# Gathered rows used by VectorE behind the split of the next block's U, with six gather buffers instead of five

## The chip, the core and the metric

The kernel runs on one core of a Trainium2 chip. The metric is the device time of one execution in microseconds. The kernel before has a median of 1936.19 us over three runs (1919.65 to 1936.87). The trace is of one more execution, with a time of 1931.02 us. TensorE (PE in the rows) multiplies, VectorE (DVE) does elementwise work, ScalarE (ACT) casts and evaluates functions, GpSimd (POOL) issues the gathers, and SyncE (SP) issues the plain loads.

## The reference

One decoder block on 512 tokens of width 1024: adaLN and RMSNorm, differential attention and mLSTM side by side, an output projection, and then a PEER feed-forward. Only the last matters here:

```
q = (h @ w_q) per head; v_top, i_top = top_k(q . sub_keys, 16) on two halves of 128 keys
sc, sel = top_k(all 256 sums, 16);  idx = the chosen experts (of 16384);  gate = softmax(sc)
act = gelu(einsum('thed,td->the', U[idx], h))
y   = einsum('the,thed->td', gate * act, V[idx])
```

Every token has 8 heads times 16 choices, so 128 rows of U and 128 rows of V, each row 1024 numbers wide. The output is x + gt2 * y, normalised.

## The kernel before

The 512 tokens are four tiles of 128. The feed-forward treats them in two ways.

**Dense, for tiles 1 to 3 (384 tokens).** All 16384 experts are computed in 128 blocks of 128 experts. `up(n1)` loads a 128x1024 block of U (`raw_U`, L990), ScalarE casts it to a rounded part `hi_U` (L991), VectorE subtracts to get the rest `lo_U` (L992, the split of U), and TensorE does 24 matmuls of 384 columns, three for each of eight slices: hi by hi (L1000), hi by the activations' low part (L1001), lo by hi (L1002). ScalarE takes the gelu (`ga`, L1004). The second half of a block loads and splits a block of V in the same way (`hi_V`, `lo_V`, helper `split`, L137 and L138), VectorE multiplies `ga` by the routing weights (L1031), `ga` is split too (`ahi`, `alo`), and TensorE does 18 matmuls of 512 columns (L1046), which add up in PSUM over all 128 blocks. `hi` and `lo` tiles of U and V have two buffers each, `ga` has 32, so the U half may run up to 32 blocks ahead of the V half.

**Gathered, for tile 0 (128 tokens).** The experts' rows are fetched instead: one indirect DMA on GpSimd's queue (L925) brings, for choice s, one row of 1024 floats to each of the 128 partitions (512 KB). With a row of U, VectorE takes the dot product with the token's activations (L931). After all 128 there is one gelu and one multiplication by the gates, and then each row of V is added to `yg`, weighted (L941). There are 256 gathers, 128 of U and then 128 of V. `gstep` spreads them over blocks 16 to 126 of the dense loop, two or three to a block (256 over 111 blocks). The choices of tile 0 are made by `select_gather` at blocks 3 and 5, with scratch tiles from the same pool of buffers as the gathers (tag `g`, `NGB` buffers of 4 KB to a partition). At the end, a last low part and three tiles of the closing normalisation come from that pool as well.

**What sets the order.** The program is written in one order, and a planner (`schedule_with_timeline_sim=True`) simulates the engines with modelled durations and writes out each engine's list: an instruction that is ready in its simulation goes ahead of one that isn't, and among ready ones the one that was written earlier. On the chip each engine works through its list in order, and waits in front of an instruction whose inputs are late. `tc.issue_after(x)` orders those instructions of its block which run on the engine of `x` behind `x`; it adds no semaphore. In `up`, GpSimd copies one column of `lo_U` (`pace`, L994), and the gathers of that block stand behind this copy on GpSimd's list, so they don't start before the block's split. Nothing orders their uses on VectorE but their data and the planner.

Of the kernel before, what the change touches and what calls it, by code (L numbers as in the profile page):

```python
# [10 lines left out]
F32 = mybir.dt.float32  # L11
# [6 lines left out]
OP = mybir.AluOpType  # L18
# [10 lines left out]
KEYS = 128  # L29
# [11 lines left out]
    (O_QA + hp * 256,), (O_KA + hp * 256,), (O_VA + hp * 256,), (O_QM + hp * 128, O_KM + hp * 128),  # L41
    (O_VM + hp * 256,), (O_OM + hp * 256,), (O_GM + hp * 256,), (O_GA + hp * 256,))]
NGA = 32
NGB = 5
QB = 1
RB = 6
STB = 2
# [14 lines left out]
def block_kernel(ctx: ExitStack, tc: tile.TileContext, a, out, dbg=None):  # L62
    nc = tc.nc
    dbg = dbg or {}
    V, A, G, T = nc.vector, nc.scalar, nc.gpsimd, nc.tensor
# [58 lines left out]
    def wtiles(kind, name, raw=None):  # L124

        return (raw or wpool.tile([P, D], F32, tag=f"w_raw{kind}", bufs=2, name=f"raw_{name}"),
                wpool.tile([P, D], F32R, tag=f"w_hi{kind}", bufs=2, name=f"hi_{name}"),
                wpool.tile([P, D], F32R, tag=f"w_lo{kind}", bufs=2, name=f"lo_{name}"))
# [15 lines left out]
    def acc_tile(name):  # L144
        return ps_acc.tile([P, 512], F32, tag="acc", name=name)
# [83 lines left out]
    with tc.tile_pool(name="start", bufs=1, side="right") as sp:  # L229
# [55 lines left out]
        for half in range(2):  # L285
# [4 lines left out]
            for k in ks:  # L290
# [3 lines left out]
                                                       op=OP.subtract)  # L294
# [423 lines left out]
    NS = NH * TOPK  # L718
# [204 lines left out]
    def gather(src, s):  # L923
        t_ = gpool.tile([P, D], F32, tag="g", bufs=NGB, name="gath")
        G.indirect_dma_start(out=t_, out_offset=None, in_=src,  # L925
                             in_offset=bass.IndirectOffsetOnAxis(ap=idx0[:, s:s + 1], axis=0))
        return t_

    def gather_u(s):
        u = gather(a["U"], s)  # L930
        V.scalar_tensor_tensor(junk2, u, 1.0, hrow, op0=OP.mult, op1=OP.mult, accum_out=act[:, s:s + 1])  # L931
        if s == NS - 1:
            A.activation(act, act, AF.Gelu)
            V.tensor_tensor(act, act, gate0, op=OP.mult)

    def gather_v(s):
        v = gather(a["V"], s)
        if s == 0:
            V.tensor_scalar(yg, v, act[:, 0:1], None, op0=OP.mult)
        else:  # L940
            V.scalar_tensor_tensor(yg, v, act[:, s:s + 1], yg, op0=OP.mult, op1=OP.add)  # L941

    def select_gather(h0):

        room = gpool.tile([P, D], F32, tag="g", bufs=NGB, name="room")
        s0 = gpool.tile([P, D], F32, tag="g", bufs=NGB, name="s0")
        used, made = [0], {}

        def mk(name, shape, dt=F32):
            n = int(np.prod(shape[1:])) * (2 if dt == F16 else 4) // 4  # L950
            if name in ("ge", "stp"):
                t_, n0 = gpool.tile([P, D], F32, tag="g", bufs=NGB, name=name), 0
            elif name == "cand":
# [19 lines left out]
        for h in range(4):  # L973
            for p in range(2):
# [2 lines left out]
        V.scalar_tensor_tensor(idx0[:, gs], idg.rearrange("p h k -> p (h k)"), float(KEYS),  # L977
                               idl.rearrange("p h k -> p (h k)"), op0=OP.mult, op1=OP.add)

    gsteps = [(gather_u, s) for s in range(NS)] + [(gather_v, s) for s in range(NS)]  # L980
    h_hi, h_lo = h2_hi[:, :, d0:d0 + XT], h2_lo[:, :, d0:d0 + XT]

    def gstep(n1):
        return min(2 * NS, max(0, (n1 - G0) * 2 * NS // (KEYS - GE - G0)))

    def up(n1):

        raw, hi, lo = wtiles(0, f"U{n1}", gpool.tile([P, D], F32, tag="rawU", bufs=NRU, name="raw_U")
                             if n1 >= NGA + 4 else None)
        nc.sync.dma_start(raw, a["UT"][n1])  # L990
        A.copy(hi, raw)  # L991
        V.tensor_tensor(lo, raw, hi.bitcast(F32), op=OP.subtract)  # L992
        pace = dp.tile([P, 1], F32, tag="pace", bufs=4, name="pace")
        with tc.issue_after(G.tensor_copy(pace, lo[:, 0:1].bitcast(F32)).ins):  # L994
            for f, s in gsteps[gstep(n1):gstep(n1 + 1)]:
                f(s)
        ps = acc_tile("act")[:, 0:XT]
        for k in range(KD):
            ks = slice(k * P, (k + 1) * P)
            T.matmul(ps, hi[:, ks], h_hi[:, k], start=(k == 0), stop=False)  # L1000
            T.matmul(ps, hi[:, ks], h_lo[:, k], start=False, stop=False)  # L1001
            T.matmul(ps, lo[:, ks], h_hi[:, k], start=False, stop=(k == KD - 1))  # L1002
        ga = dp.tile([P, XT], F32, tag="ga", bufs=NGA, name="ga")
        A.activation(ga, ps, AF.Gelu)  # L1004
        return ga
# [3 lines left out]
    for n1 in range(KEYS):  # L1009
        if n1 in SG:  # L1010
            select_gather(4 * SG.index(n1))
        for u in range(n1, n1 + 1) if n1 < KEYS - SKEW else range(n1, KEYS) if n1 == KEYS - SKEW else ():
            gas[u] = up(u)
# [18 lines left out]
        if n1 == KEYS - 1:  # L1032
            both = gpool.tile([P, D], F32R, tag="g", bufs=NGB, name="ahl")
            ahi, alo = both[:, 0:XT], both[:, XT:2 * XT]
# [15 lines left out]

    gt2 = gpool.tile([P, D], F32, tag="g", bufs=NGB, name="gt2")
    nc.sync.dma_start(gt2, gt2_dram.partition_broadcast(P))
# [81 lines left out]
```

## Time and profile before

| | |
|---|---|
| runs | 1936.19 us median, 1919.65 to 1936.87 |
| the profiled execution | 1931.02 us, span 1929.2 us |
| TensorE busy | 1814.1 us, 94% |
| VectorE busy | 1428.4 us, 74% |
| ScalarE busy | 811.1 us, 42% |
| GpSimd busy | 685.8 us, 36% |
| DMA | 404 MB, 210 GB/s on average |
| gathers of U, of V | 1052.6 to 1409.9 us, 1411.1 to 1890.3 us |

Times in rows count from the start of the span. The share of busy time is a mean over stages with different limits, so the stretch in which the gathers run has to be read apart from the rest. A bracket at the end of a row of the timeline is the time for which the engine stood idle in front of that instruction, and what ended it.

### The profile page before, as it was taken

To read this page: it belongs to the slowest core of one execution; us is meant where nothing else is said; L and a number is where in the kernel's file an instruction comes from. 1 tells how busy PE (TensorE), PEld (TensorE's weight loads), DVE (VectorE), ACT (ScalarE), POOL (GpSimd) and SP (SyncE) were. 2 spreads that over 40 slices of the span, in tenths; PEclk is the share of its full clock that TensorE was granted. 3 is DMA by queue.
4 is the path that set the end of the run, shared out by engine and by line. 5 is a ranking of instruction groups with operands and counts; after the bars stand their busy time and mean duration, and the time that the engine had idled before them with its cause. 6 is when DMAs were issued, how large, how long until landed. Compare 5 with 4: busy or idle time off the path is not lost.

```text
span 1929.2 us, 28915 instructions
## 1 busy us (share of the span) xinstructions
PE 1814.1 (94%) x10751; PEld 1632.3 (85%) x10751; DVE 1428.4 (74%) x2732; ACT 811.1 (42%) x1359; POOL 685.8 (36%) x608
## 2 busy tenths in 40 slices
PE   5999899899998998999699999999999899999997
PEld 4989799798986888999688888899898788888886
DVE  7664746645556799999889888887776667776777
ACT  5565464463562423555434333333333233333332
POOL 2523325234135310331001664565433433334333
PEclk8999999999999999999799999999999999999999
DMA  8422414314222233366794999999986887787883
GB/s 283 129 69 81 138 59 158 112 63 148 71 88 98 75 102 99 117 239 247 265 302 153 339 355 349 317 337 336 323 285 247 276 299 274 273 295 246 321 283 132
DMA packets 160283, 404.26 MB, mean 210 GB/s; under 512 B 14471, under 2 KB 63368, under 8 KB 160142
## 3 DMA queue, kind: packets, MB, share of 16 engines
q1 hardware_dynamic: 117026, 240.91, 38.6%
q0 software_dynamic: 36864, 134.23, 19.0%
q10 hardware_dynamic: 6252, 27.28, 3.6%
q8 instruction: 84, 1.38, 0.3%
q14 instruction: 57, 0.47, 0.1%
HBM read 373.52 MB, written 28.84 MB: 209 GB/s over the span
## 4 chain that ended last, share of the span: by engine, by line
PE 58%; DVE 18%; DMA 9%; ACT 5%; issue 5%; POOL 4%; SPq 0%; DVEq 0%; POOLq 0%; ACTq 0%
PE y L1046 20%; PE act L1002 7%; PE act L1000 7%; PE act L1001 7%; DMA gath<-V,idx 4%; DMA ada_w<-ada_w 3%; POOL gath L925 2%; DVE lo_U L992 2%; DVE ada_acc L219 1%; DVE lo_V L138 1%; PE wps L876 1%; PE wps L877 1%; DVE ga L699 1%; ACT p L489 1%; DVE gm L701 1%
## 5 line engine op out<-in xcount | busy, mean ns | idle before, releaser
L1002 PE MATMUL act<-h_hi,lo_U 128*128 128x384 f32 x1024 | 347.1, 339 | 16.9 <-DVE lo_U L992 16.7
L1000 PE MATMUL act<-h_hi,hi_U 128*128 128x384 f32 x1024 | 345.0, 337 | 2.6 <-ACT ga L1004 2.2
L1001 PE MATMUL act<-h_lo,hi_U 128*128 128x384 f32 x1024 | 344.3, 336 | 0.0
L994 POOL COPY pace<-lo_U 128x1 f32<-128x1 f32 x128 | 99.9, 782 | 572.8 <-DVE lo_U L992 572.1
L941 DVE SCALAR_TENSOR_TENSOR yg<-gath,act,yg 128x1024 f32<-128x1024 f32 x127 | 163.0, 1283 | 111.2 <-DMA gath<-V,idx 110.6
L1046 PE MATMUL y<-lo_V,ahi 128*128 128x512 f32 x762 | 241.2, 397 | 2.6 <-DVE lo_V L138 2.6
L137 ACT CAST hi_V<-raw_V 128x1024 fp32r<-128x1024 f32 x128 | 134.3, 1050 | 245.9 <-PE y L1046 207.3
L1046 PE MATMUL y<-hi_V,alo 128*128 128x512 f32 x762 | 233.9, 395 | 1.0 <-DVE alo L138 1.0
L1046 PE MATMUL y<-hi_V,ahi 128*128 128x512 f32 x762 | 222.4, 397 | 6.0 <-ACT ahi L137 4.2
L925 POOL DMA_INDIRECT gath<-U,idx x128 | 177.1, 1383 | 130.1 <-DVE junk L931 99.3
L1002 PEld LDWEIGHTS act<-h_hi,lo_U 128*128 128x128 f32 x1024 | 192.8, 188 | 25.3 <-DVE lo_U L992 20.6
L1000 PEld LDWEIGHTS act<-h_hi,hi_U 128*128 128x128 f32 x1024 | 192.9, 188 | 8.5 <-ACT ga L1004 3.1
L1001 PEld LDWEIGHTS act<-h_lo,hi_U 128*128 128x128 f32 x1024 | 192.7, 188 | 4.3
L138 DVE TENSOR_TENSOR lo_V<-raw_V,hi_V 128x1024 fp32r<-128x1024 f32 x128 | 155.8, 1219 | 41.9 <-ACT hi_V L137 39.0
L991 ACT CAST hi_U<-raw_U 128x1024 fp32r<-128x1024 f32 x128 | 134.2, 1049 | 111.4 <-PE act L1001 98.6
L137 ACT CAST ahi<-ga 128x384 fp32r<-128x384 f32 x127 | 65.0, 512 | 271.0 <-DVE ga L1031 140.3
L1046 PEld LDWEIGHTS y<-hi_V,alo 128*128 128x128 f32 x762 | 142.5, 187 | 35.4 <-DVE alo L138 1.9
L1046 PEld LDWEIGHTS y<-lo_V,ahi 128*128 128x128 f32 x762 | 142.8, 188 | 35.0 <-DVE lo_V L138 3.6
L992 DVE TENSOR_TENSOR lo_U<-raw_U,hi_U 128x1024 fp32r<-128x1024 f32 x128 | 156.4, 1222 | 19.4 <-ACT hi_U L991 13.3
L1046 PEld LDWEIGHTS y<-hi_V,ahi 128*128 128x128 f32 x762 | 142.0, 189 | 33.3 <-ACT ahi L137 4.8
L925 POOL DMA_INDIRECT gath<-V,idx x128 | 149.4, 1167 | 35.3 <-issue 31.5
L931 DVE SCALAR_TENSOR_TENSOR junk<-gath,hrow 128x1024 bf16<-128x1024 f32 x128 | 156.0, 1219 | 4.4 <-DMA gath<-U,idx 3.5
(465 smaller groups left out, 4134.2 us busy)
## 6 DMA issues: line engine op xcount, KB each, us to landing
raw_U<-UT SPq DMA_DIRECT2D x128, 512.0 KB
raw_V<-V SPq DMA_DIRECT2D x128, 512.0 KB
ada_w<-ada_w SPq DMA_DIRECT2D x96, 256.0 KB
W_dram<-st ACTq DMA_DIRECT2D x24, 960.0 KB
W<-W_dram SPq DMA_DIRECT2D x60, 384.0 KB
raw_wq<-wq SPq DMA_DIRECT2D x16, 512.0 KB
raw_q<-w_in SPq DMA_DIRECT2D x8, 512.0 KB
raw_k<-w_in SPq DMA_DIRECT2D x8, 512.0 KB
```

The source lines that it names most:

```text
L137: A.copy(hi, src)
L138: eng.tensor_tensor(lo, src, hi.bitcast(F32), op=OP.subtract)
L925: G.indirect_dma_start(out=t_, out_offset=None, in_=src, in_offset=bass.IndirectOffsetOnAxis(ap=idx0[:, s:s + 1], axis=0))
L931: V.scalar_tensor_tensor(junk2, u, 1.0, hrow, op0=OP.mult, op1=OP.mult, accum_out=act[:, s:s + 1])
L941: V.scalar_tensor_tensor(yg, v, act[:, s:s + 1], yg, op0=OP.mult, op1=OP.add)
L991: A.copy(hi, raw)
L992: V.tensor_tensor(lo, raw, hi.bitcast(F32), op=OP.subtract)
L994: with tc.issue_after(G.tensor_copy(pace, lo[:, 0:1].bitcast(F32)).ins):
L1000: T.matmul(ps, hi[:, ks], h_hi[:, k], start=(k == 0), stop=False)
L1001: T.matmul(ps, hi[:, ks], h_lo[:, k], start=False, stop=False)
L1002: T.matmul(ps, lo[:, ks], h_hi[:, k], start=False, stop=(k == KD - 1))
L1046: T.matmul(ys[d][j], l[:, tsl], r[:, j * 512:(j + 1) * 512], start=(m == 0 and i == 0), stop=(m == KEYS - 1 and i == 2))
```

## The change

The gather of a row and its use on VectorE are taken apart. `up(n1)` now issues its block's gathers and puts them into a list, `landing`. The next `up` empties that list right after its own split of U, inside `issue_after` on that split, so a block's uses stand behind the next block's `lo_U` on VectorE's list. In the last block the list is emptied once more at the end. The pool `g` gets a sixth buffer.

```diff
-NGB = 5
+NGB = 6
...
-    def gather_u(s):
-        u = gather(a["U"], s)
+    def use_u(s, u):
         V.scalar_tensor_tensor(junk2, u, 1.0, hrow, op0=OP.mult, op1=OP.mult, accum_out=act[:, s:s + 1])
...
-    def gather_v(s):
-        v = gather(a["V"], s)
+    def use_v(s, v):
...
-    gsteps = [(gather_u, s) for s in range(NS)] + [(gather_v, s) for s in range(NS)]
+    gsteps = [(f, n, s) for f, n in ((use_u, "U"), (use_v, "V")) for s in range(NS)]
+    landing = []
...
-        V.tensor_tensor(lo, raw, hi.bitcast(F32), op=OP.subtract)
+
+        with tc.issue_after(V.tensor_tensor(lo, raw, hi.bitcast(F32), op=OP.subtract).ins):
+            while landing:
+                f, s, t_ = landing.pop(0)
+                f(s, t_)
         pace = dp.tile([P, 1], F32, tag="pace", bufs=4, name="pace")
         with tc.issue_after(G.tensor_copy(pace, lo[:, 0:1].bitcast(F32)).ins):
-            for f, s in gsteps[gstep(n1):gstep(n1 + 1)]:
-                f(s)
+            for f, n, s in gsteps[gstep(n1):gstep(n1 + 1)]:
+                landing.append((f, s, gather(a[n], s)))
+        if n1 == KEYS - 1:
+            while landing:
+                f, s, t_ = landing.pop(0)
+                f(s, t_)
```

## Rows read from the trace of the kernel before

**Rows 1.** Stretches of gathered U and V: length, busy us (count) by engine, clock, DMA.
```profile
1052.00:1411.00 359.00, 357.77 (x1726) 313.51 (x1725) 297.10 (x445) 130.98 (x177) 196.84 (x159) 1.00 0.93 329
1411.00:1900.00 489.00, 472.97 (x2353) 423.48 (x2352) 344.01 (x354) 161.70 (x223) 180.29 (x184) 1.00 0.81 280
```

**Rows 2.** The same stretches, line 1046 alone (PE, PEld).
```profile
1052.00:1411.00 359.00, 238.03 (x969) 180.28 (x967) 1.00 0.93 329
1411.00:1900.00 489.00, 241.97 (x993) 185.26 (x994) 1.00 0.81 280
```

**Rows 3.** Timeline of TensorE: start, duration; L1000 starts every third matmul.
```profile
1508.38 0.34 PE L1000 MATMUL act<-h_hi,hi_U 128*128 128x384 f32 x1
...
1512.55 0.33 PE L1000 MATMUL act<-h_hi,hi_U 128*128 128x384 f32 x1
```

**Rows 4.** The chain of work that ended last, in order of time: start, duration.
```profile
1526.25 1.23 DVE lo_U L992
1528.14 2.30 POOL gath L925
1530.74 8.50 DMA gath<-V,idx
1540.54 1.22 DVE lo_V L138
...
1547.93 4.19 PE y L1046 x18
```

**Rows 5.** Waits from 1411 to 1900 us: total us, times, longest.
```profile
DVE yg L941 <- DMA gath<-V,idx: 110.6, 66, 5.1
...
PE act L1002 <- DVE lo_U L992: 12.8, 7, 4.7
```

**Rows 6.** Timeline of VectorE: start, duration, idle before it.
```profile
1513.06 1.28 DVE L941 SCALAR_TENSOR_TENSOR yg<-gath,act,yg 128x1024 f32<-128x1024 f32 x1
...
1539.34 1.28 DVE L941 SCALAR_TENSOR_TENSOR yg<-gath,act,yg 128x1024 f32<-128x1024 f32 x1 [3.39 <-DMA gath<-V,idx]
...
1541.67 1.22 DVE L992 TENSOR_TENSOR lo_U<-raw_U,hi_U 128x1024 fp32r<-128x1024 f32 x1
...
1544.94 1.23 DVE L992 TENSOR_TENSOR lo_U<-raw_U,hi_U 128x1024 fp32r<-128x1024 f32 x1 [0.45 <-ACT hi_U L991]
...
1549.47 1.29 DVE L941 SCALAR_TENSOR_TENSOR yg<-gath,act,yg 128x1024 f32<-128x1024 f32 x1 [1.71 <-DMA gath<-V,idx]
```

**Rows 7.** Timeline of ScalarE, the cast ahead of the split at 1541.67.
```profile
1533.99 1.04 ACT L991 CAST hi_U<-raw_U 128x1024 fp32r<-128x1024 f32 x1
```

**Rows 8.** Timeline of TensorE around its longest wait in this stretch.
```profile
1537.88 0.34 PE L1001 MATMUL act<-h_lo,hi_U 128*128 128x384 f32 x1
1542.95 0.69 PE L1002 MATMUL act<-h_hi,lo_U 128*128 128x384 f32 x1 [4.73 <-DVE lo_U L992]
```

**Rows 9.** The 3.3 us after that wait, columns as in the first group.
```profile
1543.00:1546.30 3.30, 3.30 (x10) 3.30 (x11) 2.28 (x4) 1.85 (x3) 2.37 (x4) 0.50 0.88 309
```

**Rows 10.** Timeline of GpSimd: two gathers of V.
```profile
1513.34 2.30 POOL L925 DMA_INDIRECT gath<-V,idx  x1 [0.16 <-issue]
...
1543.56 0.97 POOL L925 DMA_INDIRECT gath<-V,idx  x1 [0.16 <-issue]
```

**Rows 11.** The gathers by tile: issue in ns (min/median/max), first and last start.
```profile
L925 POOL DMA_INDIRECT gath<-U,idx x128: 932/1282/4195, 1052.6 to 1409.9; - x128
...
L925 POOL DMA_INDIRECT gath<-V,idx x128: 933/963/3903, 1411.1 to 1890.3; - x128
```

**Rows 12.** Splits of U in each stretch: busy us, mean ns, idle before.
```profile
L992 DVE TENSOR_TENSOR lo_U<-raw_U,hi_U 128x1024 fp32r<-128x1024 f32 x32 | 39.1, 1221 | 8.2 <-PE act L1002 3.3 <-ACT hi_U L991 2.9 <-issue 1.1
L992 DVE TENSOR_TENSOR lo_U<-raw_U,hi_U 128x1024 fp32r<-128x1024 f32 x56 | 68.3, 1220 | 11.7 <-ACT hi_U L991 10.4 <-PE act L1002 1.0 <-issue 0.3
```

**Rows 13.** Waits from 1052 to 1411 us: total us, times, longest.
```profile
POOL gath L925 <- DVE junk L931: 99.3, 78, 6.5
...
ACT hi_V L137 <- DMA raw_V<-V: 10.4, 4, 7.4
```

## The prediction

> **What bounds the kernel now.** I read the stretches first, then TensorE's pace, then the chain of waits, then who waits there, and last the timelines.
>
> By stretches, TensorE is busy 357.8 of 359 us while rows of U are gathered, and 473.0 of 489 us while rows of V are [rows 1]. Busy isn't full pace, so I count matmuls. A U block's 24 take 4.17 us at full pace (eight steps of three [rows 3]), a V block's 18 take 4.19 us [rows 4]. In the V stretch 993 of 2353 matmuls are line 1046 [rows 1, 2]: 55.2 V blocks and 56.7 U blocks, 231.2 + 236.3 = 467.5 us. So TensorE loses **21.5 us** of 489. In the U stretch 969 and 757 give 225.6 + 131.5 = 357.1 us, a loss of 1.9 of 359. The kernel is bound by TensorE, and what a change of the gathers can give back there is at most 23 us, 1.2%.
>
> The chain shows what costs those 21.5 us: a circle [rows 4]. A split of U ends, GpSimd issues that block's gathers behind it (2.30 us for one), the row lands 8.50 us later, and only then come the next split of V and the next split of U. VectorE takes its list in order, so a use that stands ahead of a split holds the split until the row is there. This costs VectorE 110.6 us in 66 waits, and TensorE 12.8 us in seven waits for `lo_U` [rows 5]. In the worst one VectorE waited 3.39 us in front of the use at 1539.34; the split of U at 1541.67 [rows 6] had its cast ready from 1535.0 [rows 7]; TensorE, which had started its last matmul at 1537.88, stood until 1542.95 [rows 8]. Afterwards the granted clock was 0.50, the lower level of 1.2 GHz, for 3.3 us with ten matmuls [rows 9], which take 10 x 0.174 = 1.7 us at full pace [rows 3]: 1.6 us more. That use belongs to the block whose split stands at 1526.25 [rows 4], so it is exactly one that the change puts behind the split at 1541.67.
>
> **The change part by part.**
>
> *Uses behind the next split.* No instruction is added or taken away; on VectorE 256 uses move, and what stands behind them moves up. In the case above the split of V is free to start after its own cast and the split of U from 1535.0; two splits of 1.22 us [rows 6] end by about 1537.5, and TensorE needs the result at 1538. The wait goes. I let all seven go, with the clock's part: 12.8 + 1.6 = **14.4 us**. Above it lies the whole loss of 21.5 us, below it nothing; I take 14.4 because the rows name its cause, while the other 7.1 us are shorter gaps for which `lo_U` isn't named.
>
> *What stays.* The splits come in pairs: 1541.67 and 1544.94 [rows 6]. A use of the first one's rows already stands behind the second split: the gather issued at 1543.56 [rows 10] is used at 1549.47 after a wait of 1.71 us [rows 6], 5.9 us after its issue. The change can't move that one. Only the second block of each pair, about 28 of 56 [rows 12], gets its rows a whole pair's time to land, 16.7 us (2 x 8.36). What is late next is this first use, with the splits of V behind it.
>
> *The wait that is added.* It is an order on VectorE alone, without a semaphore. Behind a late split now stand its predecessor's uses; who waits for these are the gathers that need their buffers. Two blocks in a row hold at most five (256 over 111 blocks), so with six the next block's gathers always find one. I cost it at 0, covered by VectorE's 145 us of idle time in the V stretch (489 - 344 [rows 1]).
>
> *GpSimd's list.* The gathers stay behind `pace`, 256 of them before and after, no DMA is added, and SyncE's list doesn't change. Cost 0.
>
> *Six buffers in the U stretch.* Here the order isn't binding: of 128 splits 56 + 32 come later [rows 12], so 40 were done when block 16's gathers started at 1052.6 [rows 11]; the uses lag far behind. But GpSimd waited 99.3 us for buffers [rows 13], and the sixth lets gathers go up to 6/5 as fast. They move 128 x 0.524 MB in 359 us, 187 of 329 GB/s [rows 1]; a fifth more makes 366 GB/s, and the DMA share 0.93 would go to 1.03. The next loads of V could then come late. From above: ScalarE's waits for `raw_V`, 10.4 us [rows 13], twice as long and all on TensorE, +10 us. From below: this stretch's loss gone, -1.9 us. I take 0, since TensorE lost just 1.9 us here with the DMA this full.
>
> *Scratch and tail.* A sixth buffer may let the second `select_gather` start sooner, and the closing loads too. Between 0 and 2 us of gain, as the tail after the last gather's use is short; I take 0.
>
> **Sum.** 1931.0 - 14.4 = 1916.6 us against the profiled execution. That one stands 5.2 us below the median of the runs shown, so the same step from the median gives 1921.8. I predict the middle, **1919 us**, 0.9% below the median. One per cent, 19.4 us, is about what a measurement of this kernel can tell from no change: the bounds are 1916.8 and 1955.6.
>
> **The rivals.**
>
> *The whole loss goes.* If rows that land late feed the shorter gaps too, TensorE gets 23.4 us back: 1907.6, from the median 1912.8, say 1910. For it speaks that nothing else in the V stretch is near full; against it that half of the uses don't move.
>
> *Given back.* Uses now follow a split directly, which is when GpSimd, released by `pace`, issues the block's gathers. A gather's issue has a median of 0.963 us in the V stretch and 1.282 us in the busier U stretch [rows 11], and the one at 1513.34 beside the use at 1513.06 took 2.30 us [rows 6, 10]. If each gather took 2.30 - 0.96 = 1.34 us more, a block's rows (2.31 on average) would land 3.1 us later, and for the first block of each of 28 pairs VectorE would wait 87 us more. Of its waits 14.4/110.6, 13%, have reached TensorE: 11.3 us. That leaves 3 us of gain: 1928. The crowded DMA of the U stretch would end in the same place (1916.6 + 10 = 1927). The Trainium skill, SBUF — State Buffer, section "Who interferes with whom", has a rule that speaks for this rival: a VectorE instruction with two SBUF inputs and a GpSimd instruction that reads SBUF share a port, and the later one is blocked until the first is done. The trace agrees in kind: the gather of 2.30 us began 0.28 us after the use and ended 1.30 us after it, about its own undisturbed length [rows 6, 10].
>
> *Nothing happens.* The planner already sets half of the uses behind the next split, and might set the splits of V behind the waiting uses all the same: 1931 to 1936.
>
> *Slower.* The place is between the two splits of a pair. The uses are written ahead of everything that follows the split, so the planner may put up to three of 1.28 us there, 2.96 us on average. The two splits are 3.27 us apart now [rows 6], then 6.23 us; TensorE's U block takes 4.17. From the point at which they are further apart than that, and no V block lies between to fill in, TensorE waits up to 2.06 us a pair, 58 us over 28 pairs: 1931 - 14 + 58 = 1975. For it speaks the order of writing; against it that V blocks do lie between and that the planner starts those first in its simulation.
>
> **How the numbers follow.** Forecast 42% (its own range 1908 to 1930), whole loss 14%, given back 20%, nothing 11%, slower 13%. Faster by over 1% holds the whole-loss case and four tenths of the forecast: 0.14 + 0.17 = 0.31. Slower by over 1% is the last case, but for a little of it: 0.12. The rest, 0.57, is within 1%. The range from 1904 to 1942 takes in all but the slower case and a few per cent at the ends.
>
> **What would show it.** In the V stretch `yg`'s wait for gathered rows should fall from 110.6 to about half, TensorE's waits for `lo_U` from 12.8 us to under 3, and the pace of matmuls should rise to some 2353 in 475 us, with VectorE's busy time the same. The gathers' issue should stay near 0.96 us; if its median goes over 1.3, it is the port. In the U stretch TensorE should still lose about 2 us; if `raw_V` is waited for longer, the sixth buffer has a price. The prediction is wrong if the planner gives up the pairs, so that the stretch is no longer the same one, or if the loss lay in gaps that no gathered row feeds.

## The result, and the profile after

The changed kernel takes **1909.51 us** (median of 10 runs, 1904.74 to 1915.96), against 1936.07 for the kernel before in runs beside it (10 runs, 1919.65 to 1942.41). The ratio is **0.9876, 95% interval 0.9852 to 0.9901**: faster by 1.2%, some 24 us by this ratio (26.6 us by the medians). The profiled executions differ by nearly as much: 1908.75 against 1931.02 us, spans 1907.0 and 1929.2.

The stretches of the kernel after come first, as in [rows 1, 2]: all engines, then line 1053 (its matmuls of V) alone. The second window ends at 1895, since TensorE's last matmul ends at 1894.9.

```profile
1052.00:1411.00 359.00, 358.45 (x1727) 313.86 (x1726) 300.04 (x447) 130.29 (x177) 200.77 (x161) 1.00 0.93 331
1411.00:1895.00 484.00, 483.01 (x2414) 433.85 (x2412) 353.29 (x372) 168.16 (x236) 194.31 (x184) 1.00 0.82 281
...
1052.00:1411.00 359.00, 240.11 (x976) 181.65 (x975) 1.00 0.93 331
1411.00:1895.00 484.00, 257.58 (x1050) 195.20 (x1048) 1.00 0.82 281
```

The same window of the kernel before, for a like comparison (line 1046 in the second row):

```profile
1411.00:1895.00 484.00, 467.97 (x2329) 419.03 (x2328) 341.62 (x352) 161.21 (x222) 180.29 (x184) 1.00 0.81 279
...
1411.00:1895.00 484.00, 238.97 (x980) 182.65 (x980) 1.00 0.81 279
```

Counted as in the prediction (18 matmuls of V in 4.19 us, 24 of U in 4.17), 1050 and 1364 matmuls are 481.4 us of work, so TensorE loses **2.6 us** of 484; before it was 980 and 1349, 462.5 us, a loss of **21.5**. In the U stretch the loss went from 1.9 to 1.3. These two make 19.5 us of the 22.3 between the profiles; the other 2.8 lie ahead of 1052 and behind 1895. The tail behind TensorE's last matmul, 12.0 us before and 12.1 after, has no part in them.

The waits from 1411 to 1900 of the kernel after (total us, times, longest), which answer to [rows 5]:

```profile
DVE lo_V L138 <- ACT hi_V L137: 62.8, 22, 5.1
DVE yg L939 <- DMA gath<-V,idx: 50.4, 32, 3.9
...
DVE lo_U L992 <- ACT hi_U L990: 6.9, 11, 1.6
...
PE y L1053 <- ACT hi_V L137: 0.8, 3, 0.3
```

VectorE still waits 50.4 us for rows, but TensorE's only wait is 0.8 us for a cast; it no longer waits for `lo_U`. VectorE instead stands in front of splits of V whose cast isn't made, that is, it is early. The chain that ended last was a circle through a split, GpSimd, a gather and VectorE [rows 4]; on the page of after it is followed back only to 1715.9 us, and from there it is nearly all TensorE:

```profile
PE 9%; DVE 1%; issue 0%; DVEq 0%; POOLq 0%; POOL 0%; ACT 0%
```

On the pages of five and pairs_late, two kernels of the next section, it goes back through the whole span. The gathers of V, 4% of the chain of the kernel before, are not among the entries listed there.

VectorE's timeline in the kernel after (start, duration, idle before), beside [rows 6]:

```profile
1496.43 1.23 DVE L992 TENSOR_TENSOR lo_U<-raw_U,hi_U 128x1024 fp32r<-128x1024 f32 x1
1497.57 1.28 DVE L939 SCALAR_TENSOR_TENSOR yg<-gath,act,yg 128x1024 f32<-128x1024 f32 x1
1498.77 0.55 DVE L1038 TENSOR_TENSOR ga<-ga,W 128x384 f32<-128x384 f32 x1
...
1500.59 1.23 DVE L992 TENSOR_TENSOR lo_U<-raw_U,hi_U 128x1024 fp32r<-128x1024 f32 x1
...
1505.65 1.22 DVE L992 TENSOR_TENSOR lo_U<-raw_U,hi_U 128x1024 fp32r<-128x1024 f32 x1
...
1513.80 1.28 DVE L939 SCALAR_TENSOR_TENSOR yg<-gath,act,yg 128x1024 f32<-128x1024 f32 x1 [1.88 <-DMA gath<-V,idx]
...
1521.53 1.23 DVE L992 TENSOR_TENSOR lo_U<-raw_U,hi_U 128x1024 fp32r<-128x1024 f32 x1
```

Two things are seen. A use follows a split directly and stands ahead of the product `ga*W` (line 1038). And the **pairs are gone**: splits of U come in groups of three, at 1496.43, 1500.59 and 1505.65, the next group 25.1 us later. Two differences could thus be the cause, the place of the uses and the grouping, besides the buffer.

### The profile page after: what moved, and what is told of

It reads as the page before. It is cut to its first block, busy times and chain, and to the rows that moved or that the text cites. A ratio compares the mean times of both kernels' runs of the same rounds, so it can differ in the third digit from the quotient of the medians.

```text
span 1907.0 us, 28945 instructions
## 1 busy us (share of the span) xinstructions
PE 1806.2 (95%) x10751; PEld 1628.1 (85%) x10751; DVE 1423.5 (75%) x2732; ACT 811.6 (43%) x1359; POOL 708.5 (37%) x608
## 5 line engine op out<-in xcount | busy, mean ns | idle before, releaser
L997 POOL COPY pace<-lo_U 128x1 f32<-128x1 f32 x128 | 115.0, 900 | 546.5 <-DVE lo_U L992 546.3
L1053 PE MATMUL y<-hi_V,alo 128*128 128x512 f32 x762 | 229.9, 395 | 0.0
L1053 PE MATMUL y<-hi_V,ahi 128*128 128x512 f32 x762 | 216.9, 397 | 4.9 <-ACT ahi L137 3.5
L939 DVE SCALAR_TENSOR_TENSOR yg<-gath,act,yg 128x1024 f32<-128x1024 f32 x127 | 162.8, 1282 | 50.6 <-DMA gath<-V,idx 50.4
## 6 DMA issues: line engine op xcount, KB each, us to landing
W<-W_dram SPq DMA_DIRECT2D x60, 384.0 KB, 10.8
```

What stands on the lines that cost most here:

```text
L1053: T.matmul(ys[d][j], l[:, tsl], r[:, j * 512:(j + 1) * 512], start=(m == 0 and i == 0), stop=(m == KEYS - 1 and i == 2))
```

## The experiments

Four theories are told apart. **Held split**: a use that waits for its row holds the splits behind it, and the change takes the uses from in front of them. **Buffers**: the sixth buffer lets rows be there earlier. **Regrouping**: the planner's groups of three are the gain. **Price of the place**: a use directly behind a split delays what follows it. The table has all timed kernels; the loss is TensorE's in the windows 1052 to 1411 and 1411 to 1895, counted as above (for ahead the windows no longer hold one stretch each); the wait is VectorE's for rows of V from 1411 to 1900; the intervals are of 95%. A loss or a wait is that of one execution, and two executions of the same kernel differ by up to some 5 us there. Each ratio is to runs of the kernel before beside that kernel.

```
kernel        ratio to before            median us  loss U, V us   wait us
before        1                          1936.07     1.9   21.5    110.6
before_again  (one run)                  1935.11     0.5   26.6    113.6
after         0.9876 (0.9852 to 0.9901)  1909.51     1.3    2.6     50.4
after_again   0.9880 (0.9857 to 0.9902)  1910.95     5.4    0.6     45.4
five          0.9895 (0.9862 to 0.9927)  1910.90     7.3    0.5     49.7
six_alone     0.9934 (0.9910 to 0.9957)  1918.25     0.6   11.0     88.6
seven_alone   0.9956 (0.9937 to 0.9974)  1924.17    12.9    9.6     87.4
no_v_use      0.9883 (0.9852 to 0.9914)  1909.66     6.5   -0.2     38.0
two_back      0.9887 (0.9864 to 0.9910)  1911.35     2.9    0.9      1.4
pairs_plain   0.9991 (0.9969 to 1.0013)  1932.03     0.3   27.2    112.5
pairs         1.0109 (1.0085 to 1.0132)  1954.96     2.7   42.9     78.2
pairs_late    0.9896 (0.9877 to 0.9915)  1913.61     0.4    3.1      2.3
late          0.9876 (0.9854 to 0.9898)  1909.48     2.3    0.7      3.9
ahead         1.2315 (1.2258 to 1.2373)  2380.84   110.8  154.0     89.8
```

**Six buffers alone** (before, `NGB = 5` to `6`).

> The kernel before with six gather buffers and nothing else; the planner still has pairs of blocks. Held split (a use whose row is late holds up the next split of U or V): the uses stay ahead of the next splits, so VectorE's wait for gathered rows in the V stretch stays near 110 us and the time near 1931 to 1936, within 0.3% of before. Buffers (the sixth buffer is what helps): near 1910, ratio 0.987.

```profile
DVE yg L941 <- DMA gath<-V,idx: 88.6, 57, 4.8
...
PE act L1002 <- DVE lo_U L992: 6.8, 5, 2.1
```

Neither theory had this right: about half of the gain is there with the uses where they were. The circle is weaker, not gone: TensorE still waits for `lo_U` five times. The planner also wrote another list with six buffers (VectorE's order in the trace is not that of the kernel before), so even this run doesn't show the buffer by itself.

**The order alone** (after, `NGB = 6` to `5`).

> The changed kernel with five gather buffers. Held split: two blocks in a row hold at most five rows, so the gain stays whole, 1907 to 1914, ratio 0.986 to 0.990, and GpSimd waits a little longer for buffers. Buffers: the gain goes, 1930 or more.

With the order, five buffers do in the V stretch what six do: loss 0.5 us, wait 49.7. The loss of 7.3 us in the U stretch stands beside 10.8 us in one wait of ScalarE for `raw_V`, but after_again shows 5.4 us there with six, so that is not a price of the fifth buffer that these runs can tell.

**Rows of V hardly used** (before).

```
-            V.scalar_tensor_tensor(yg, v, act[:, s:s + 1], yg, ...)
+        elif s % 8 == 7:
+            V.tensor_scalar(yg[:, 0:1], v[:, 0:1], act[:, s:s + 1], None, ...)
```

> The kernel before with five buffers, in which VectorE reads only one element of every eighth gathered row of V (the weighted sum over the rows is left out); all gathers stay, and the planner's list still has pairs of blocks. Held split: with next to nothing waiting for rows TensorE keeps full pace in pairs too, 1907 to 1914, and its waits for lo_U fall from 12.8 to under 3 us. Regrouping (groups of three blocks in the planner's new lists are what gives TensorE slack): pairs stay slow, 1922 or more.

Splits in pairs and five buffers are kept, and TensorE's loss in the V stretch is zero within the count (-0.2 us). All 21.5 us hung on VectorE's uses of rows of V; this includes the gaps that the prediction had left where they were. The run takes VectorE's work on these rows away together with the waits (127 uses of 1.28 us), so by itself it doesn't tell the two apart; five does, where all of the work stays and the loss is 0.5 us.

**The opposite order** (after; the next split stands behind the waiting uses).

```
-        with tc.issue_after(V.tensor_tensor(lo, raw, hi..., op=OP.subtract).ins):
-            while landing: ...
+        while landing:
+            f, s, t_ = landing.pop(0)
+            last = f(s, t_)
...
+            with tc.issue_after(last.ins):
+                V.tensor_tensor(lo, raw, hi..., op=OP.subtract)
```

> The changed kernel with the edge turned round: the split of the next block's U stands behind the uses of this block's rows, six buffers. Held split: every split now waits for the rows of the block before; issue and landing take some 8 us after a split's end, so two splits can't be closer than about 12 to 14 us where TensorE needs 8.4 a block: 50 to 56 blocks times 4 to 5 us, 200 to 280 us slower, 2130 to 2210. Regrouping: the place of the uses matters little, 1925 to 1950.

```profile
PE act L1015 <- DVE lo_U L1001: 45.4, 17, 4.7
PE y L1059 <- ACT ahi L137: 38.1, 14, 6.6
```

Right in sign and too small in size: 449 us more by the medians, not 200 to 280. The work is so far behind that rows of U are still used at 1524 us, so both stretches pay. The granted clock fell with the gaps, to a mean of 0.913 (0.981 after). A split that must wait for its predecessor's rows is what costs time.

**Pairs kept** (after; TensorE's U block n behind V block n-2 from block 76).

```
+        with ExitStack() as behind:
+            if n1 >= 76 and n1 - 2 in vlast:
+                behind.enter_context(tc.issue_after(vlast[n1 - 2].ins))
             for k in range(KD): ...
```

> The changed kernel, six buffers, with an edge on TensorE as well: from block 76 on, the U matmuls of block n stand behind the V matmuls of block n-2, so the planner can't make groups of three blocks and stays with pairs. Held split: all uses still stand behind the next split, so 1907 to 1914 and about the changed kernel's time on this chip. Regrouping: back to the kernel before, 1925 or more.

The time came out slower than before, as regrouping would have it, but the trace shows another reason. VectorE, then ScalarE, then TensorE of this kernel:

```profile
1503.82 1.23 DVE L992 TENSOR_TENSOR lo_U<-raw_U,hi_U 128x1024 fp32r<-128x1024 f32 x1 [0.94 <-ACT hi_U L990]
1504.96 1.28 DVE L939 SCALAR_TENSOR_TENSOR yg<-gath,act,yg 128x1024 f32<-128x1024 f32 x1
1506.16 0.55 DVE L1042 TENSOR_TENSOR ga<-ga,W 128x384 f32<-128x384 f32 x1
...
1507.79 0.51 ACT L137 CAST ahi<-ga 128x384 fp32r<-128x384 f32 x1
...
1508.35 0.74 PE L1057 MATMUL y<-hi_V,ahi 128*128 128x512 f32 x2 [1.37 <-ACT ahi L137]
```

The use at 1504.96 follows the split of U and delays `ga*W`; its cast `ahi` comes after TensorE wants it. This happens 25 times:

```profile
PE y L1057 <- ACT ahi L137: 36.9, 25, 1.7
```

**Its control** (the same order on TensorE, uses where the kernel before has them).

> Six buffers and the pairs on TensorE (U of block n behind V of block n-2 from block 76), but the uses stand where the kernel before has them, not behind the split. It is the control for the kernel with pairs, which took 1954.96. Price of the place (the use that follows a split of U directly stands ahead of ga*W, and TensorE waits for the cast behind that product): without those uses the waits of TensorE for ahi go from 36.9 us to under 5 and the time is that of six buffers alone, 1912 to 1925, ratio 0.99 to 0.996. Rival, the order on TensorE itself costs: 1945 to 1960, ratio over 1.006, with ahi waits of over 25 us.

```profile
DVE yg L939 <- DMA gath<-V,idx: 112.5, 56, 4.8
...
PE y L1057 <- ACT ahi L137: 21.2, 19, 1.7
```

This lies between the two cases: a loss of 27.2 us, with 21.2 us of `ahi` waits and no use held behind a split. VectorE, then TensorE, around one of these waits:

```profile
1515.17 1.28 DVE L939 SCALAR_TENSOR_TENSOR yg<-gath,act,yg 128x1024 f32<-128x1024 f32 x1 [4.51 <-DMA gath<-V,idx]
1517.26 1.28 DVE L939 SCALAR_TENSOR_TENSOR yg<-gath,act,yg 128x1024 f32<-128x1024 f32 x1 [0.80 <-DMA gath<-V,idx]
...
1524.38 0.55 DVE L1042 TENSOR_TENSOR ga<-ga,W 128x384 f32<-128x384 f32 x1
...
1525.53 0.72 PE L1057 MATMUL y<-hi_V,ahi 128*128 128x512 f32 x2 [1.39 <-ACT ahi L137]
```

Uses that waited for their rows have made VectorE late, and TensorE now meets the delay at `ahi` instead of `lo_U`. VectorE had stood for rows in the 15 us ahead of `ga*W` in all 19 cases, and in only one does a use stand directly between the split and `ga*W`. So this is the held list once more, and the place directly behind the split adds 15.7 us. That the order on TensorE costs nothing like 27 us by itself is seen next.

**Pairs, with the uses behind `ga*W`** (blocks 76 to 122).

```
-            while landing:
+            while landing and not 76 <= n1 < KEYS - SKEW:
...
-        V.tensor_tensor(g3, g3, W[...], op=OP.mult)
+        with tc.issue_after(V.tensor_tensor(g3, g3, W[...], op=OP.mult).ins):
+            for _ in range(dues[n1] if ... else 0): f, s, t_ = landing.pop(0); f(s, t_)
```

> The kernel with pairs, but from block 76 to block 122 the gathered rows are used behind the next block's ga*W product instead of directly behind its split. Price of the place: the waits for ahi go, rows have even longer to land, 1906 to 1916, ratio 0.986 to 0.992, as the kernel after, although the pairs are kept. Rival, pairs cost whatever the place of the uses is: 1940 or more.

```profile
1501.06 1.22 DVE L992 TENSOR_TENSOR lo_U<-raw_U,hi_U 128x1024 fp32r<-128x1024 f32 x1
1502.19 0.55 DVE L1044 TENSOR_TENSOR ga<-ga,W 128x384 f32<-128x384 f32 x1
1502.66 1.28 DVE L939 SCALAR_TENSOR_TENSOR yg<-gath,act,yg 128x1024 f32<-128x1024 f32 x1
...
1505.53 1.22 DVE L992 TENSOR_TENSOR lo_U<-raw_U,hi_U 128x1024 fp32r<-128x1024 f32 x1
1506.66 0.55 DVE L1044 TENSOR_TENSOR ga<-ga,W 128x384 f32<-128x384 f32 x1
```

The list of waits has no wait of TensorE left in this stretch. The edits of the three kernels with the same order on TensorE differ only in where the uses stand: as before 1932.0 us, directly behind the split 1955.0, behind `ga*W` 1913.6 (the kernel before in the runs beside them 1933.2, 1933.1 and 1933.2). **Regrouping isn't needed for the gain**, and the place has a price where TensorE takes U and V in pairs. The order on TensorE as such has next to none: this kernel loses 3.1 us in the V stretch.

**The same place without the order on TensorE** (after, uses behind `ga*W`, blocks 76 to 122).

> The kernel after without any order on TensorE, but with the uses from block 76 to block 122 behind the next block's ga*W product instead of directly behind its split. If the kernel after still loses by its place (the use ahead of ga*W) or by rows that land late, this is faster: 1904 to 1907, ratio 0.984 to 0.986. If, as I think, groups of three hide the place and VectorE's remaining waits for rows cost TensorE nothing, it is the same: 1907 to 1913, ratio 0.987 to 0.990.

The same as the kernel after: in groups of three, the use ahead of `ga*W` costs nothing that can be measured. Why groups of three bear it is not shown.

**Uses behind the next but one split** (after; seven buffers, two for raw U).

```
-            while landing:
-                f, s, t_ = landing.pop(0)
+            while landing and landing[0][0] < n1 - 1:
+                _, f, s, t_ = landing.pop(0)
```

> The changed kernel with the uses behind the split of the next block but one, seven gather buffers, and two buffers instead of three for raw_U to make room. Held split: VectorE's wait for rows in the V stretch falls from 50 us to near 0, but TensorE has only about 6 us left to lose there, so the time stays within 0.3% of the changed kernel, 1903 to 1912. Were VectorE's waits themselves a cost (13% of them, as in the kernel before), another 6 us would come off; if two raw_U buffers are too few, it gets slower.

```profile
DVE yg L939 <- DMA gath<-V,idx: 1.4, 3, 0.9
```

VectorE's waits for rows went from about 50 to 1.4 us, and the time stayed. What is left of them in the kernel after costs TensorE nothing. late, with three buffers for raw U, says the same: 3.9 us of waits and the same time.

**Seven buffers alone** (before, `NGB = 7`, and `NRU = 2` to make room).

> The kernel before with seven gather buffers (and two of the buffers for raw U instead of three, to make room), uses where they were. If more buffers as such let rows be there earlier and this gave back half of the loss with six, a seventh gives back more or at least as much: 1908 to 1920, ratio 0.988 to 0.994, VectorE's wait for rows in the stretch of V below 89 us. If the gain with six was a chance of the order that the planner came to: anywhere from 1915 to 1936, with 47 of 128 uses still without a split of U between, and a wait of 90 to 115 us.

Both theories missed a part. In the V stretch a seventh buffer does what the sixth does (loss 9.6 and 11.0, wait 87.4 and 88.6), which speaks against chance; but it adds nothing there, and the U stretch loses 12.9 us, with 14.0 us of ScalarE's waits for `raw_V`. Seven buffers or two for raw U: not told apart.

**Both kernels once more.**

> The changed kernel once more, beside the others of this call. 1905 to 1914, ratio to before 0.986 to 0.991.

> The kernel before, a second profile, to see how much of its loss in the V stretch is the same from one execution to the next. Held split: time and loss go together; TensorE's waits for lo_U are among the largest losses again, 8 to 20 us, and its loss in the stretch is 18 to 28 us for a time between 1925 and 1940.

after_again gave 0.9880. before_again took 1935.11 us:

```profile
DVE yg L941 <- DMA gath<-V,idx: 113.6, 62, 5.9
...
PE act L1002 <- DVE lo_U L992: 13.2, 9, 2.8
```

The waits are those of [rows 5], and the worst one is shorter (2.8 against 4.7), yet TensorE loses 26.6 us in the V stretch. Most of the difference is the clock. The granted clock was at the lower level once in that stretch of the first profile [rows 9], and four times here, each time behind a wait of TensorE of 1.9 to 2.8 us:

```profile
1497.00:1500.30 3.30, 3.30 (x12) 3.30 (x12) 2.29 (x3) 1.84 (x4) 2.56 (x3) 0.50 0.86 250
1684.70:1688.00 3.30, 3.30 (x12) 3.30 (x11) 2.28 (x4) 1.79 (x3) 2.37 (x4) 0.50 0.93 317
1739.30:1742.60 3.30, 3.30 (x12) 3.30 (x11) 2.51 (x4) 0.94 (x2) 3.14 (x2) 0.50 0.81 211
1879.30:1882.60 3.30, 3.30 (x10) 2.56 (x9) 3.27 (x3) 0.00 (x0) 0.00 (x0) 0.50 0.57 163
```

Each fall cost about 1.5 us, an estimate from the starts of ten matmuls of U, 0.32 us apart instead of 0.17; three more make 4.5 of the 5.1 us. The execution on which the sum was made had few of them, and so a rather small loss.

## Why the prediction was right or wrong

The time lies in the range, 9.5 us below the predicted one, and in the forecast's own range. But the rival **the whole loss goes** (1910, given 14%) describes what happened better than the forecast, and a gain of over 1%, which came, had been given 0.31 against 0.57 for less than 1% either way.

*Luck had a part.* The prediction reckoned with pairs. In the one kernel where this change stands with pairs (forced on TensorE, and so not quite the planner's own), it takes 1955 us, outside the range. The planner's change to groups of three, which the forecast had not reckoned with, kept the measured time inside.

*What bounds the kernel: right.* TensorE's loss of 21.5 us in the V stretch held the gain, and the circle made it: no_v_use takes the uses away, and the loss with them.

*The step that was mis-sized: the gain of the uses' new place, 14.4 us.* It is 18.9 us in the V stretch (21.5 - 2.6), and 21.0 in five, where the number of buffers is left as it was. The sum stopped at the waits that name `lo_U`. Before, the same stretch has three more waits of TensorE, which the prediction passed over:

```profile
PE y L1046 <- DVE lo_V L138: 1.4, 1, 1.4
PE y L1046 <- DVE alo L138: 1.0, 1, 1.0
PE y L1046 <- ACT ahi L137: 0.7, 1, 0.7
```

Two name VectorE, one a cast that needs VectorE's product, and none is left after. With these 3.1 us the sum would have been 17.5. Most of the remaining 4.0 of 21.5 isn't in other, shorter gaps, as the prediction had it, but at the same ten waits, as TensorE's starts show:

```profile
1494.24 0.34 PE L1001 MATMUL act<-h_lo,hi_U 128*128 128x384 f32 x1
1496.05 0.44 PE L1002 MATMUL act<-h_hi,lo_U 128*128 128x384 f32 x1 [1.48 <-DVE lo_U L992]
1496.34 0.34 PE L1000 MATMUL act<-h_hi,hi_U 128*128 128x384 f32 x1
```

Two steps take 2.10 us here and 0.35 at full pace: 1.75 us are lost, where the row says 1.48. At 0.27 us each, an estimate from this one, ten waits cost 2.7 us more than their rows say. The whole loss of TensorE was the better estimate than the waits that name one tile.

*What stays, half of the uses: it is more than half, although the number for the wait came true.* The wait did fall to about half (110.6 to 50.4). But on VectorE's list of the kernel before just 47 of the 128 uses of rows of V stand with no split of U between their own block's and themselves, not half of them; after the change none does. (These are counts over the whole trace, the gathers matched to their uses in order.) The uses that the change moves were the ones that cost time. "What is late next", a use with splits of V behind it, did come (the 1.88 us at 1513.80, for one), but those waits cost TensorE nothing (two_back, late).

*The pairs.* The prediction said that it would be wrong if the planner gave up the pairs. It gave them up, and the gain came all the same; pairs_late shows that it doesn't rest on that.

*The slower rival: its place is real.* Uses directly behind a split were priced as delaying the second split of a pair. What they delay is `ga*W` and `ahi`, 1.37 us in the wait shown, 36.9 us in all, and with the pairs kept the kernel is slower than before (1955; the rival said 1975). The planner's groups of three hide it. At 13% this was weighed fairly, for another reason than given.

*Given back: no.* The gathers by tile in the kernel after, beside [rows 11]:

```profile
L925 POOL DMA_INDIRECT gath<-U,idx x128: 933/1336/2061, 1045.0 to 1403.4; - x128
...
L925 POOL DMA_INDIRECT gath<-V,idx x128: 933/1102/2298, 1404.6 to 1863.9; - x128
```

The median issue in the V stretch rose from 0.963 to 1.102 us, a tenth of the 1.34 us that the rival charged, and under its mark of 1.3. Its mechanism shows on GpSimd's `pace`:

```profile
1497.72 1.17 POOL L997 COPY pace<-lo_U 128x1 f32<-128x1 f32 x1 [11.31 <-DVE lo_U L992]
...
1506.93 0.44 POOL L997 COPY pace<-lo_U 128x1 f32<-128x1 f32 x1 [0.39 <-DVE lo_U L992]
```

`pace` takes 0.19 us while VectorE is idle (at 1518.43 in the kernel before), 0.44 beside a short product and 1.17 beside a use: it ends at 1498.89, the use at 1498.85. The Trainium skill, SBUF — State Buffer, section "Who interferes with whom", says that a VectorE instruction with two SBUF inputs contends with a GpSimd instruction that reads SBUF, and that the port which they share is locked by one of them at a time. The trace agrees for `pace`, and the delay stays on GpSimd; that the gathers' longer issue has the same cause is not shown.

*Buffers at 0: right with the order, wrong without it.* five and after can't be told apart; six_alone gained 0.66%. In the U stretch the sixth buffer didn't hurt: ScalarE's wait for `raw_V` was 10.4 us before [rows 13], and 7.6 and 10.8 in the two profiles after. The Trainium skill, Perfetto Trace Analysis, section "Optimization Strategy", says that the same gap coming again and again can mean too few buffers. Were that the whole cause here, six alone would have closed the gaps; it halved them, and the order closed them with five.

*Open.* Why the sixth buffer alone halves the loss. GpSimd waited for a buffer in the V stretch of the kernel before for only 3.8 us in two waits, and 49 uses (48 with seven) still have no split between, as 47 before. Buffer and rewritten list are not told apart.

No version ran faster than the changed kernel: late is the same within the intervals.

## What to carry to other kernels

On an engine that takes its list in order, a use that may wait for a transfer belongs behind whatever the bounding engine needs next, and "next" is every product on that path: behind the split alone the same move cost 1.1% in one order of TensorE's work and gave 1.2% in another, behind `ga*W` it gave 1.0 and 1.2%. For the size of the gain, look at the bounding engine's whole loss in the stretch, counted from its instructions, and not only at the waits that name one tile. Then test it twice: take the waiting work away, as no_v_use does, and keep the work and change its order alone, as five does.

## What was not expected of the hardware

- A VectorE wait of 50 us in a stretch was worth nothing: 50.4, 3.9 and 1.4 us of it (after, late, two_back) go with 1909.5, 1909.5 and 1911.4 us.
- The runs of the kernel before lie 22.8 us apart (10 runs), those of two_back 1.2 us (5 runs) and of pairs_late 2.0 us (5 runs). That the circle makes the scatter is not shown: the kernel after, without it, has 11.2 us in 10 runs, and seven_alone, with it, 7.8 in 11.
